# Values computed in pairs, early groups reordered, and some weight sums made by transfers

## The chip, the cores and the metric

The kernel runs on one core of one Trainium2 chip. The metric is the time of one execution on the device in microseconds (us); the time shown for a kernel is the median of several runs. All matrix products run in float32r on TensorE (PE). VectorE (DVE) and ScalarE (ACT) prepare operands and do the rest of the arithmetic, GpSimd (POOL) does a few small operations, and SyncE (SP) issues the loads.

## The reference, cut to what matters

The input x has 256 rows of 4096 numbers. One layer is computed:

```
xn   = rms_norm(x)
proj = xn @ w_in                      # 4096 x 14336, split into q, k, v, z_a, a, g, z_c (2048 columns each)
y_a  = rms_norm(chunked_attention(q, k, v, rel_table)) * silu(z_a)      # 16 heads of 128
u    = causal depthwise conv, 31 taps, of a * sigmoid(g)
y_c  = rms_norm(silu(layer_norm(u)) @ w_pw + b_pw) * silu(z_c)
h    = x + concat(y_a, y_c) @ w_out
h    = h + sigmoid(rms_norm(h) @ w_ple_gate + b) * (p @ w_ple)
out  = rms_norm(h)
```

## The kernel before

**Products.** Rows are two halves of 128 (h), columns are blocks of 512, the inner dimension is blocks of 128. Every operand is split into a high part (cast to float32r) and a low part (the rest), and each product is three matmuls: high x high, low x high, high x low. Weights are split on the core: ACT casts the high part (L204), DVE subtracts to get the low part (L205); both are made in `parts_of`.

**Units.** `mixed_product` computes two column blocks at a time. A unit is a pair of inner blocks. A plain unit takes 2 x 2 x 2 products of three matmuls, 24 in all. A unit marked `*` replaces eight products by seven (21 matmuls), in the manner of Strassen: it needs sums of the weight blocks, `ua` (two column-wise sums, L426 and L427) and `ub` (two more built on `ua`, L430 and L431), which are made on DVE, cast and split like weights (`pair_parts`), and matching combinations of the activations (`comb`, `xS`). The seven products go into the four accumulators and into four helper banks P1, P5, P6, P7, which are all four temporary banks of PSUM (`ps_tmp`). After the last seven of an order, `on_helpers` adds the helpers up. The orders are written by hand as text, such as `early`, with the `*` units among the plain ones.

**Fills.** Work with time to spare is queued in `later`: convolution taps (L677), the steps of the layer norm over the convolution, combinations. After each unit of a product, `fill(n)` takes n of them; the counts stand in `early_fills`, one for each unit. A compile-time scheduler then fixes each engine's order, mainly by program order and by the readiness that its model gives.

**Order of the first half.** `glu_conv(c)` computes a and g for 512 columns as a pair and queues 124 taps. `heads(g)` computes q and k for four heads as a pair (`scaled_pair`, q and k 2048 columns apart), turns both into head layout (`to_heads`), then computes v for these heads as one block of 512 columns with `product` (L218: no seven-product units, 192 matmuls), then `attention`. The order is conv group 0, then for g = 0, 1, 2: conv group g+1 and heads g; then the layer norm is queued and heads 3 follow. Before the last v product, the pool for sums (`upool`) is closed and a pool (`more`) takes its place, which holds the split operand of the pointwise product (`uS`). The pointwise product follows, with the orders "1 3 4 5 0* 6 2* 7" and plain.

**Attention** of one group runs four heads one after the other: scores on PE (L848, L849), bias, maximum and exponential on DVE and ACT (L855 to L860), transposes (L867), the product with v (L872 to L874), scaling into `y_a` (L876). Each head takes three banks from `ps_tmp`. The bias tile is loaded by SP at the start of `heads` and then partly overwritten by POOL (L895).

**Buffers that matter.** Weight tiles: 5 (`wpool`); their high and low parts: 3 each; `u` tiles and their parts: 2 each; tag `hd` (bias, kT, v, convolution inputs, layer norm scratch): 5; `ps_tmp` banks: 4. SP loads weights in order, each load waiting for a free tile.

Of the kernel before, what the change touches and what calls it, by code (L numbers as in the profile page):

```python
# [3 lines left out]

# [21 lines left out]
def hybrid_block(  # L26
# [23 lines left out]
    nc = tc.nc  # L50
# [113 lines left out]
    def transposed(src, blocks, then=lambda ins: None):  # L164

        pt = tmp_psum()
        for i, b in enumerate(blocks):
            for h in range(NH):
                last_transpose[:] = [
                    nc.tensor.transpose(  # L170
                        pt[:, i * T + h * P : i * T + (h + 1) * P],
                        src[:, h, b * P : (b + 1) * P],
                        ident,
                    )
                ]
                then(*last_transpose)
        return [pt[:, i * T : (i + 1) * T] for i in range(len(blocks))]
# [21 lines left out]
    def parts_of(wt, kc, tiles=None):  # L199
        if tiles is None:  # L200
            tiles = part_tiles()
        wh, wl = tiles
        made = (
            nc.scalar.copy(wh[:, :kc, :], wt[:, :kc, :]),  # L204
            nc.vector.tensor_tensor(  # L205
                wl[:, :kc, :], wt[:, :kc, :], wh[:, :kc, :].bitcast(F32), ALU.subtract
            ),
        )
        return (wh, wl), made

    def accumulate(acc, h, lhs, kb, wh, wl, k, kblocks, then=lambda ins: None):
        t, i = lhs[kb // 4], kb % 4
# [99 lines left out]

    def units(text):

        return [(int(u.rstrip("*")), u.endswith("*")) for u in text.split()]


    dense = units("1 0* 3 2* 5 4* 6* 7 8* 9 10* 11 12* 14* 13 15")
    first = units("0 1 3 5 7 9 11 13 15 2* 8 4* 10 6* 12 14")
    early = units("1 3 5 7 0* 9 2* 11 4* 13 6* 15 8 10 12 14")  # L320
    early_six = units("1 3 5 7 0* 9 2* 11 4* 13 6* 15 8* 10* 12 14")

    early_fills = (4, 6, 7, 1, 5, 1, 5, 1, 5, 1, 2, 4, 6, 6, 6, 4)
    final = units("1 0* 3 2* 5 4* 6* 7 8* 9 10* 12* 11 13 14 15")
    late = units("1 3 5 7 9 11 13 15 0* 2 4* 6 8* 10* 12 14")

    def mixed_product(
# [54 lines left out]
        def add_plain(n, k, wh, wl, **kw):  # L382
            pair = order[n][0]
            for j in range(2):
                for h in range(NH):
                    name = (("P2", "P3"), ("P4", "X"))[h][j]
                    add(name, block(2 * pair + k, h), (wh[:, j], wl[:, j]), n, k == 1, **kw)

        done, after = 0, ExitStack()
        if begin:  # L390
            done, behind = begin(add_plain)
# [3 lines left out]
        for n, (pair, seven) in enumerate(order):  # L395
# [4 lines left out]
            wts = []  # L400
            for k in range(2):
                wt = wpool.tile([P, 2, NB], F32, tag="w", name="wt")
                nc.sync.dma_start(wt, two_columns(w, 2 * pair + k, col, apart))
# [18 lines left out]
            ua = upool.tile([P, 2, NB], F32, tag="u", name="ua")  # L422
            ub = upool.tile([P, 2, NB], F32, tag="u", name="ub")
            plus = partial(nc.vector.tensor_tensor, op=ALU.add)
            w0h, w0l = parts_of(w0, 1)[0]
            plus(ua[:, 0], w0[:, 0], w0[:, 1])  # L426
            plus(ua[:, 1], w0[:, 1], w1[:, 1])  # L427
            uah, ual = pair_parts(ua)
            w1h, w1l = parts_of(w1, 2)[0]
            plus(ub[:, 0], ua[:, 0], w1[:, 1])  # L430
            plus(ub[:, 1], ub[:, 0], w1[:, 0])  # L431
            ubh, ubl = pair_parts(ub)
# [37 lines left out]
        tt(z[1][0], helper["P7"], z[1][0], ALU.add)  # L470
        tt(z[1][1], helper["P5"], z[1][0], ALU.add)

    def sum_tiles():

        t = [spool.tile([P, NH, NB], F32, tag="stage", name="z") for _ in range(2)]
        return t, [[t[j][:, h] for j in range(2)] for h in range(NH)]

    def scaled_pair(w, col, apart, order, r, fills, **kw):

        t, z = [], []  # L480

        def on_helpers(helper):
            for dst, src in zip((t, z), sum_tiles()):
                dst.extend(src)
            nc.scalar.activation(z[0][0], helper["P1"], AF.Identity, scale=r[:, :1])
            helper_sums(helper, z)
            for h, j in QUARTERS[1:]:
                nc.scalar.activation(z[h][j], z[h][j], AF.Identity, scale=r[:, h : h + 1])

        c = mixed_product(w, col, xT, xS, order, on_helpers, fills=fills, apart=apart, **kw)  # L490
        for h, j in QUARTERS:
            stt(  # L492
                z[h][j], c[h][j], r[:, h : h + 1], z[h][j],
                ALU.mult, ALU.subtract if j else ALU.add,
            )
        return t

    def square_sum(dst, src, scale=1.0):
        junk = spool.tile([P, NB], mybir.dt.bfloat16, tag="junk", name="junk", bufs=1)
        return nc.scalar.activation(junk[:, : src.shape[1]], src, AF.Square, scale=scale, accum_out=dst)  # L500

    def rstd_of(partial, n, name):
        r = cpool.tile([P, partial.shape[1]], F32, name=name)
# [185 lines left out]
    def glu_conv(c):  # L689
        if c == 0:  # L690
            sg, gate = scaled_pair(
                w_in0, o_a, o_g - o_a, first, r_x, (1,), begin=first_pairs
            )
        else:
            last = c == CW // NB - 1
            sg, gate = scaled_pair(
                w_in0, o_a + c * NB, o_g - o_a, early_six if last else early, r_x, early_fills,
                ahead=more_combinations if last else None,
            )
        for h in range(NH):  # L700
# [25 lines left out]
    def layer_norm_swish():  # L726

        add = nc.vector.tensor_tensor
        st = {}

        def hd_tile(name):
            return spool.tile([P, 4, T], F32, tag="hd", name=name, bufs=5)

        def fold(s):
            add(s[:, :2, :], s[:, :2, :], s[:, 2:, :], ALU.add)
# [87 lines left out]
    y_a = []  # L823
    ssq_a = cpool.tile([P, NH, AW // NB], F32, name="ssq_a")

    def to_heads(st, name):

        t = spool.tile([P, GH, T], F32, tag="hd", name=name, bufs=5)
        for pair in range(GH // 2):
            pt = tmp_psum()  # L830
            for i in range(2):
                for h in range(NH):
                    b = 2 * pair + i
                    nc.tensor.transpose(  # L834
                        pt[:, i * T + h * P : i * T + (h + 1) * P],
                        st[:, h, b * P : (b + 1) * P],
                        ident,
                    )
# [5 lines left out]
    def attention(g, qT, kT, v, bias):  # L844
        y = act.tile([P, NH, NB], F32, tag="act", name="y_a")
        for hd in range(GH):
            sp = tmp_psum()
            nc.tensor.matmul(sp[:, :P], qT[:, hd, :P], kT[:, hd, :P], start=True, stop=True)  # L848
# [25 lines left out]
            nc.tensor.matmul(o[:, HD : 2 * HD], pT[:, 2 * P :], v[:, 1, vc], start=False, stop=True)  # L874
            for h in range(NH):
                nc.scalar.activation(  # L876
                    y[:, h, vc], o[:, h * HD : (h + 1) * HD], AF.Identity, scale=den[:, h : h + 1]
                )
        for h in range(NH):
            square_sum(ssq_a[:, h, g : g + 1], y[:, h, :])  # L880
        y_a.append(y)

    def heads(g):
        nonlocal more
        bias = spool.tile([P, GH, T], F32, tag="hd", name="bias", bufs=5)
# [10 lines left out]
        q, k = scaled_pair(w_in0, o_q + g * NB, o_k - o_q, early, r_x, (4,) if g == n_g - 1 else early_fills)  # L896
        qT, kT = to_heads(q, "qT"), to_heads(k, "kT")
        if g == n_g - 1:
            first_sums.close()
            more = pool("more", 4)  # L900
        accv = product(w_in0, o_v + g * NB, xT, KD)
        v = spool.tile([P, NH, NB], F32, tag="hd", name="v", bufs=5)
        for h in range(NH):
            nc.scalar.activation(v[:, h, :], accv[h], AF.Identity, scale=r_x[:, h : h + 1])
        attention(g, qT, kT, v, bias)

    n_g = H // GH
    assert n_g == CW // NB
# [68 lines left out]
    def gated(ys, c0, col, r_y, order, ahead):  # L977
# [6 lines left out]

        acc = mixed_product(w_in0, col + c0 * NB, xT, xS, order, on_helpers, ahead=ahead, fills=(2,))
        for h, j in QUARTERS:
            zz, y = z[h][j], ys[c0 + j][:, h, :]
            tt(zz, acc[h][j], zz, ALU.subtract if j else ALU.add)  # L988
            nc.scalar.activation(zz, zz, AF.Silu, scale=r_x[:, h : h + 1])
            later.append(partial(stt, y, y, r_y[:, h : h + 1], zz, ALU.mult, ALU.mult))  # L990

    def before_last(make):
# [278 lines left out]
```

## Time and profile before

| | |
|---|---|
| median of 3 runs | 2038.79 us (2037.45 to 2039.75) |
| profiled execution | 2039.1 us, span 2037.3 us |
| PE busy | 2019.6 us, 9106 matmuls |
| DVE busy | 1887.9 us |
| ACT busy | 1200.8 us |
| POOL busy | 8.1 us, 19 instructions |
| moved by transfers | 412.29 MB |

The span is the time from the first to the last instruction of the one profiled execution; around it lie 1.8 us of that execution's own time. Engine times overlap. A line such as L370 is the line of the kernel's file; `acc` and `acc_P` are the accumulators and the helper banks of `mixed_product`, `wh` and `wl` high and low parts of weights, `uh` and `ul` those of the sums. PEld is PE's weight load.

### The profile page before, as it was taken

The page shows a single profiled execution, that of the slowest core. Times are in us where ns is not written, and L with a number is a line of the kernel's source. Part 1 is how long each engine was busy: PE and PEld are TensorE (multiplying, and loading weights), DVE is VectorE, ACT ScalarE, POOL GpSimd, SP SyncE. Part 2 cuts the span into 40 slices and gives each one's busy share as a digit, 9 for nine tenths or more (in the row PEclk, how much of TensorE's full clock was granted, in tenths as well). Part 3 has the DMA queues.
Part 4 walks back from the last instruction along what each step waited for, and adds up shares of the span by engine and source line. Part 5 has one row for each costly group of instructions (what it writes and reads, how often), then busy time and mean ns, then how long its engine had stood idle before and what let it go on. Part 6 is the DMA issues. An engine that isn't in the chain of part 4 may idle for free.

```text
span 2037.3 us, 26041 instructions
## 1 busy us (share of the span) xinstructions
PE 2019.6 (99%) x9106; PEld 1659.5 (81%) x9106; DVE 1887.9 (93%) x2688; ACT 1200.8 (59%) x1559; POOL 8.1 (0%) x19
## 2 busy tenths in 40 slices
PE   9999999999999999999999999999999999999997
PEld 7888888877888888888888888888888888888876
DVE  7999999799989998868899999999999999999998
ACT  7655546554565546676555656676565666655555
POOL 0000000000000000000000000000000000000000
PEclk9999999999999999999999999999999999999999
DMA  8666665666656665655666666676666656666765
GB/s 295 188 200 204 204 187 165 202 191 189 184 185 204 201 188 183 186 184 199 190 216 204 197 216 199 219 238 204 214 201 205 214 185 208 198 221 205 235 208 179
DMA packets 161853, 412.29 MB, mean 202 GB/s; under 512 B 12974, under 2 KB 16190, under 8 KB 161722
## 3 DMA queue, kind: packets, MB, share of 16 engines
q1 hardware_dynamic: 161072, 409.80, 63.3%
q8 instruction: 71, 1.16, 0.2%
q10 hardware_dynamic: 650, 0.84, 0.1%
q14 instruction: 60, 0.49, 0.1%
HBM read 406.39 MB, written 4.19 MB: 202 GB/s over the span
## 4 chain that ended last, share of the span: by engine, by line
PE 86%; DVE 10%; issue 2%; DMA 1%; ACT 1%; POOLq 0%; POOL 0%; ACTq 0%; DVEq 0%
PE acc L370 61%; PE acc_P L370 15%; PE acc L218 7%; DVE wl L205 4%; DVE cv L677 3%; DMA wt<-in_w_in_dram 1%; PE tmp_ps L170 1%; DVE ul L205 1%; PE tmp_ps L867 0%; PE tmp_ps L849 0%; ACT wh L204 0%; PE acc L358 0%; PE tmp_ps L834 0%; DVE z L492 0%; PE tmp_ps L872 0%
## 5 line engine op out<-in xcount | busy, mean ns | idle before, releaser
L370 PE MATMUL acc<-wh,big_t 128*128 128x512 f32 x3788 | 1172.1, 391 | 0.6 <-DVE z L988 0.3
L204 ACT CAST wh<-wt 128x1024 fp32r<-128x1024 f32 (+1 forms) x737 | 715.8, 982 | 543.0 <-PE acc L370 330.6
L205 DVE TENSOR_TENSOR wl<-wt,wh 128x1024 fp32r<-128x1024 f32 (+1 forms) x737 | 825.4, 1132 | 65.0 <-ACT wh L204 60.1
L370 PEld LDWEIGHTS acc<-wh,big_t 128*128 128x128 f32 x3788 | 708.4, 188 | 146.5 <-issue 0.6
L370 PE MATMUL acc<-wl,big_t 128*128 128x512 f32 x1894 | 731.1, 391 | 1.0 <-DVE wl L205 1.0
L370 PEld LDWEIGHTS acc<-wl,big_t 128*128 128x128 f32 x1894 | 355.2, 188 | 76.7 <-DVE wl L205 3.1
L677 DVE SCALAR_TENSOR_TENSOR cv<-uT,dw,cv 128x255 f32<-128x255 f32 (+23 forms) x480 | 204.9, 467 | 1.1
L204 ACT CAST uh<-ub 128x1024 fp32r<-128x1024 f32 x122 | 128.5, 1054 | 126.2 <-DVE ub L431 102.7
L218 PE MATMUL acc<-wh,big_t 128*128 128x512 f32 x560 | 173.1, 390 | 0.0
L204 ACT CAST uh<-ua 128x1024 fp32r<-128x1024 f32 x122 | 128.7, 1055 | 71.7 <-DVE ua L427 63.5
L205 DVE TENSOR_TENSOR ul<-ub,uh 128x1024 fp32r<-128x1024 f32 x122 | 149.0, 1221 | 8.8 <-ACT uh L204 7.8
L370 PE MATMUL acc_P<-uh,big_t 128*128 128x512 f32 x504 | 154.4, 392 | 0.0
L205 DVE TENSOR_TENSOR ul<-ua,uh 128x1024 fp32r<-128x1024 f32 x122 | 148.9, 1220 | 0.4 <-ACT uh L204 0.2
L218 PEld LDWEIGHTS acc<-wh,big_t 128*128 128x128 f32 x560 | 104.8, 188 | 21.4
L370 PEld LDWEIGHTS acc_P<-uh,big_t 128*128 128x128 f32 x504 | 93.3, 188 | 22.2 <-ACT uh L204 3.7
L218 PE MATMUL acc<-wl,big_t 128*128 128x512 f32 x280 | 109.1, 390 | 0.0
L426 DVE TENSOR_TENSOR ua<-wt 128x512 f32<-128x512 f32 x122 | 83.9, 688 | 25.9 <-DMA wt<-in_w_in_dram 19.0
L370 PE MATMUL acc_P<-ul,big_t 128*128 128x512 f32 x252 | 96.8, 392 | 0.0
L427 DVE TENSOR_TENSOR ua<-wt 128x512 f32<-128x512 f32 x122 | 83.7, 686 | 3.9 <-DMA wt<-in_w_in_dram 3.0
L431 DVE TENSOR_TENSOR ub<-ub,wt 128x512 f32<-128x512 f32 x122 | 83.8, 687 | 1.0
L430 DVE TENSOR_TENSOR ub<-ua,wt 128x512 f32<-128x512 f32 x122 | 83.7, 686 | 0.3
L370 PE MATMUL acc<-uh,big_t 128*128 128x512 f32 x244 | 75.4, 390 | 0.0
(241 smaller groups left out, 1523.0 us busy)
## 6 DMA issues: line engine op xcount, KB each, us to landing
wt<-in_w_in_dram SPq DMA_DIRECT2D x447, 512.0 KB, 4.0
wt<-in_w_out_dram SPq DMA_DIRECT2D x128, 512.0 KB, 4.2
wt<-in_w_ple_gate_dram SPq DMA_DIRECT2D x128, 512.0 KB, 4.2
wt<-in_w_pw_dram SPq DMA_DIRECT2D x32, 512.0 KB, 4.5
hc<-in_x_dram SPq DMA_DIRECT2D x8, 512.0 KB, 5.8
wt<-in_w_ple_dram SPq DMA_DIRECT2D x8, 512.0 KB, 4.2
xin<-in_x_dram SPq DMA_DIRECT2D x7, 512.0 KB, 8.2
out_dram<-hc SPq DMA_DIRECT2D x12, 256.0 KB, 2.4
```

The source lines that it names most:

```text
L170: nc.tensor.transpose(pt[:, i * T + h * P : i * T + (h + 1) * P], src[:, h, b * P : (b + 1) * P], ident,)
L204: nc.scalar.copy(wh[:, :kc, :], wt[:, :kc, :]),
L205: nc.vector.tensor_tensor(wl[:, :kc, :], wt[:, :kc, :], wh[:, :kc, :].bitcast(F32), ALU.subtract),
L218: nc.tensor.matmul(acc, a, b[:, k, :], start=kb == 0 and kind == 0, stop=kb == kblocks - 1 and kind == 2,)
L370: nc.tensor.matmul(banks[name], a, b, start=name not in begun, stop=final and ends[name] == n and kind == 2 and not (left and name in "P2 ...
L426: plus(ua[:, 0], w0[:, 0], w0[:, 1])
L427: plus(ua[:, 1], w0[:, 1], w1[:, 1])
L430: plus(ub[:, 0], ua[:, 0], w1[:, 1])
L431: plus(ub[:, 1], ub[:, 0], w1[:, 0])
L677: nc.vector.scalar_tensor_tensor(cv[:, i, PAD - k :], uT[:, i, : T + k - PAD], dw[:, b, k : k + 1], cv[:, i, PAD - k :], ALU.mult, ALU.add,)
```

## The change

- **Paired values.** v is no longer one column block per group with `product`. `values(g)` computes the v of groups g and g+1 as one pair with `scaled_pair`, with four seven-product units in each call. Their destination is given by `home` (for the first call the `hd` tag).
- **Order.** `heads` is taken apart into `load_bias`, `keys`, `values`, `attention`, which are now called as in the list below. Attention 2 and 3 stand together at the end, their biases are loaded inside the last values call, where the pool `more` is opened as well. Attention now writes its result over the q tile, in head layout, and later readers follow.
- **Early order.** The plain and seven-product units are mixed in another order, with other fill counts; the last conv group keeps the former counts (`six_fills`).
- **Transferred sums.** A unit marked `+` is a seven-product unit whose `ua` is not made by DVE: SP loads the shared second column block twice into `ua`, and a transfer issued by POOL adds the two other blocks onto it in the transfer (`accum_op=ALU.add`). It is asked for up to two units ahead (`sums_ahead`). The unit's first weight tile then loads one column block only, and `ub` is made in place in `ua`.
- **Queueing.** For `+` units, the cast and the low part of `ua` are put behind the last cast and low part of the preceding pair on their engines (`queued_behind`; ordering only).

```diff
-    early = units("1 3 5 7 0* 9 2* 11 4* 13 6* 15 8 10 12 14")
+    early = units("1 3 5 0+ 7 9 2+ 11 13 4+ 15 8 6+ 10 12 14")
+    valued = units("1 3 5 7 8 0+ 9 10 2+ 11 12 4+ 13 6* 14 15")
-    early_fills = (4, 6, 7, 1, 5, 1, 5, 1, 5, 1, 2, 4, 6, 6, 6, 4)
+    early_fills = (5, 6, 1, 5, 6, 1, 5, 6, 1, 5, 6, 1, 2, 5, 5, 4)
+    six_fills = (4, 6, 7, 1, 5, 1, 5, 1, 5, 1, 2, 4, 6, 6, 6, 4)
...
+    @contextmanager
+    def queued_behind(made):
+        with ExitStack() as queued:
+            for ins in made:
+                queued.enter_context(tc.issue_after(ins.ins))
+            yield
...
+        def sums_ahead(n):
+            for m in range(n, min(n + 3, len(order))):
+                if order[m][1] != "+" or m in sums:
+                    continue
+                ua = sums[m] = upool.tile([P, 2, NB], F32, tag="u", name="ua")
+                rows = w[2 * order[m][0] * P : (2 * order[m][0] + 1) * P, :]
+                step = P * rows.ap[0][0]
...
+                nc.sync.dma_start(ua, columns(col + apart, 0))
+                nc.gpsimd.dma_start(ua, columns(col, step + apart), accum_op=ALU.add)
...
+                if seven == "+" and k == 0:
+                    nc.sync.dma_start(wt[:, 0], w[2 * pair * P : (2 * pair + 1) * P, col : col + NB])
+                else:
+                    nc.sync.dma_start(wt, two_columns(w, 2 * pair + k, col, apart))
                 wts.append(wt)
+            sums_ahead(n)
...
+            before = list(recent)
             w0h, w0l = parts_of(w0, 1)[0]
-            plus(ua[:, 0], w0[:, 0], w0[:, 1])
-            plus(ua[:, 1], w0[:, 1], w1[:, 1])
-            uah, ual = pair_parts(ua)
+            if seven == "+":
+                ua = ub = sums[n]
+            else:
+                ua = upool.tile([P, 2, NB], F32, tag="u", name="ua")
+                plus(ua[:, 0], w0[:, 0], w0[:, 1])
+                plus(ua[:, 1], w0[:, 1], w1[:, 1])
+            with queued_behind(before if seven == "+" else ()):
+                uah, ual = pair_parts(ua)
...
-        y = act.tile([P, NH, NB], F32, tag="act", name="y_a")
+        y = qT.rearrange("q g (h d) -> q h g d", h=NH)
...
+    def values(g, order, fills, **kw):
+        vs[g], vs[g + 1] = scaled_pair(w_in0, o_v + g * NB, NB, order, r_x, fills, **kw)
+
+    def late_pool():
+        nonlocal more
+        first_sums.close()
+        more = pool("more", 4)
+        for g in (2, 3):
+            load_bias(g)
...
     glu_conv(0)
-    for g in range(n_g):
-        if g + 1 < n_g:
-            glu_conv(g + 1)
-        else:
-            layer_norm_swish()
-        heads(g)
+    glu_conv(1)
+    load_bias(0)
+    keys(0, early_fills)
+    values(0, early, early_fills, home=dict(tag="hd", bufs=5))
+    attention(0)
+    glu_conv(2)
+    glu_conv(3)
+    load_bias(1)
+    keys(1, early_fills)
+    attention(1)
+    keys(2, early_fills)
+    layer_norm_swish()
+    keys(3, (4,))
+    values(2, valued, (5, 5, 4, 5, 4, 1, 3, 2, 1, 3, 2, 1, 1, 6, 6, 6), then=late_pool)
+    attention(2)
+    attention(3)
```

More of the change, by code (lines that the diff above doesn't have):

```diff
@@ L387, in add_plain, with columns @@
                     add(name, block(2 * pair + k, h), (wh[:, j], wl[:, j]), n, k == 1, **kw)
+        sums = {}
+        def sums_ahead(n):
[5 more added lines that the diff above has]
+                step = P * rows.ap[0][0]
+                def columns(first, step):
+                    return bass.AP(
+                        tensor=rows.tensor, offset=rows.offset + first,
+                        ap=[list(rows.ap[0]), [step, 2], [1, NB]],
+                    )
+                nc.sync.dma_start(ua, columns(col + apart, 0))
+                nc.gpsimd.dma_start(ua, columns(col, step + apart), accum_op=ALU.add)
         done, after = 0, ExitStack()
@@ L471, in helper_sums, with sum_tiles, scaled_pair @@
         tt(z[1][1], helper["P5"], z[1][0], ALU.add)
-    def sum_tiles():
-        t = [spool.tile([P, NH, NB], F32, tag="stage", name="z") for _ in range(2)]
+    def sum_tiles(**kw):
+        kw = kw or dict(tag="stage")
+        t = [spool.tile([P, NH, NB], F32, name="z", **kw) for _ in range(2)]
         return t, [[t[j][:, h] for j in range(2)] for h in range(NH)]
-    def scaled_pair(w, col, apart, order, r, fills, **kw):
+    def scaled_pair(w, col, apart, order, r, fills, home={}, then=lambda: None, **kw):
         t, z = [], []
         def on_helpers(helper):
-            for dst, src in zip((t, z), sum_tiles()):
+            for dst, src in zip((t, z), sum_tiles(**home)):
                 dst.extend(src)
+            then()
             nc.scalar.activation(z[0][0], helper["P1"], AF.Identity, scale=r[:, :1])
@@ L696, in glu_conv @@
             sg, gate = scaled_pair(
[L697 removed]
+                w_in0, o_a + c * NB, o_g - o_a, *((early_six, r_x, six_fills) if last else (early, r_x, early_fills)),
                 ahead=more_combinations if last else None,
@@ L876, in attention, with hd_tile, load_bias @@
                 nc.scalar.activation(
-                    y[:, h, vc], o[:, h * HD : (h + 1) * HD], AF.Identity, scale=den[:, h : h + 1]
+                    y[:, h, hd], o[:, h * HD : (h + 1) * HD], AF.Identity, scale=den[:, h : h + 1]
                 )
         for h in range(NH):
-            square_sum(ssq_a[:, h, g : g + 1], y[:, h, :])
+            square_sum(ssq_a[:, h, g : g + 1], y[:, h])
         y_a.append(y)
-    def heads(g):
-        nonlocal more
-        bias = spool.tile([P, GH, T], F32, tag="hd", name="bias", bufs=5)
+    qs, ks, vs, biases = {}, {}, {}, {}
+    def hd_tile(name):
+        return spool.tile([P, GH, T], F32, tag="hd", name=name, bufs=5)
+    def load_bias(g):
+        bias = biases[g] = hd_tile("bias")
         span = 2 * MAXR + 1
@@ L895, in heads, with keys @@
         nc.gpsimd.memset(bias[: P // 2, :, : P // 2], NEG)
[L896 to L905, printed above, removed]
+    def keys(g, fills):
+        q, k = scaled_pair(w_in0, o_q + g * NB, o_k - o_q, early, r_x, fills)
+        qs[g] = act.tile([P, GH, T], F32, tag="act", name="qT")
+        to_heads(q, qs[g])
+        ks[g] = hd_tile("kT")
+        to_heads(k, ks[g])
+    def values(g, order, fills, **kw):
[6 more added lines that the diff above has]
+            load_bias(g)
     n_g = H // GH
-    assert n_g == CW // NB
+    assert n_g == CW // NB == 4
     glu_conv(0)
-    for g in range(n_g):
-        if g + 1 < n_g:
-            glu_conv(g + 1)
-        else:
-            layer_norm_swish()
-        heads(g)
+    glu_conv(1)
[14 more added lines that the diff above has]
+    attention(3)
     r_a = rstd_of(ssq_a, AW, "r_a")
```

28 lines of the change are left out of this document (15 added, 13 removed).

## The prediction

> **What bounds the kernel now.** I read the page's totals first, then the chain of waits in order of time, then what TensorE waited for, then busy time by stage.
>
> ```profile
> span 2037.3 us, 26041 instructions
> PE 2019.6 (99%) x9106; PEld 1659.5 (81%) x9106; DVE 1887.9 (93%) x2688; ACT 1200.8 (59%) x1559; POOL 8.1 (0%) x19
> PEclk9999999999999999999999999999999999999999
> PE 86%; DVE 10%; issue 2%; DMA 1%; ACT 1%; POOLq 0%; POOL 0%; ACTq 0%; DVEq 0%
> ...
> q1 hardware_dynamic: 161072, 409.80, 63.3%
> ```
>
> TensorE (PE) is busy for 2019.6 of 2037.3 us at full granted clock. So all idle time together is 17.7 us, and whatever is saved on VectorE (DVE), ScalarE (ACT) or the transfers can return at most that. The other way to save is fewer matmuls, so their price matters. One uninterrupted run in the chain gives it, the second values product:
>
> ```profile
> 499.47 43.55 PE acc L218 x192
> ```
>
> 43.55 / 192 = 0.2268 us for each matmul of 512 columns. Next, what PE waited for, by its weight loads:
>
> ```profile
> PEld acc_P L370 <- ACT uh L204: 4.7, 18, 0.5
> PEld tmp_ps L867 <- ACT s L860: 4.1, 12, 0.7
> PEld acc_P L370 <- DVE ul L205: 4.0, 14, 0.6
> PEld tmp_ps L872 <- ACT pT L869: 3.4, 11, 0.4
> PEld acc L370 <- DVE wl L205: 3.1, 7, 1.2
> PEld tmp_ps L834 <- DVE z L492: 3.1, 5, 1.7
> ```
>
> These are many short waits: 11.8 us for prepared weights (uh, ul, wl) over the whole kernel, 10.6 us inside attention and at its transposes. By stage:
>
> ```profile
> 102.00:316.00 214.00, 213.88 (x957) 175.88 (x957) 213.40 (x352) 106.33 (x117) 0.31 (x1) 1.00 0.65 199
> 860.00:904.00 44.00, 44.00 (x198) 36.50 (x197) 32.61 (x58) 31.19 (x53) 0.00 (x0) 1.00 0.62 190
> 904.00:932.00 28.00, 28.00 (x144) 22.63 (x143) 17.19 (x36) 20.20 (x45) 1.06 (x1) 1.00 0.47 156
> 58.00:1080.00 1022.00, 1018.22 (x4600) 836.10 (x4599) 928.03 (x1436) 573.79 (x744) 4.69 (x8) 1.00 0.62 192
> ```
>
> The columns are window, length, then busy us (count) of PE, PEld, DVE, ACT, POOL, then clock, DMA share and GB/s. From 102 to 316 us DVE is as full as PE (213.4 of 214), yet PE loses nothing: the convolution taps are what gets put off. Later DVE has gaps. The changed half, 58 to 1080 us, has PE idle for 3.8 us by this count. The end of the chain is PE.
>
> **Part 1: values in pairs (the only PE term).** A plain unit (two row blocks by two column blocks) is 24 matmuls, a seven-product unit 21. The four single products are 4 x 32 x 2 x 3 = 768 matmuls. Two paired calls of 16 units with four sevens each are 2 x (384 - 12) = 744. The other groups keep their counts: the early order has four sevens before and after, the last gate group keeps six. So 24 matmuls go: 24 x 0.2268 = **-5.4 us**. All of this is on the path, because PE is.
>
> Its cost lies on DVE, priced from these rows:
>
> ```profile
> L205 DVE TENSOR_TENSOR wl<-wt,wh 128x1024 fp32r<-128x1024 f32 x44 | 53.5, 1220 | 0.2 <-ACT wh L204 0.2
> L205 DVE TENSOR_TENSOR wl<-wt,wh 128x512 fp32r<-128x512 f32 x4 | 2.8, 690 | 0.0
> L205 DVE TENSOR_TENSOR ul<-ua,uh 128x1024 fp32r<-128x1024 f32 x4 | 4.9, 1222 | 0.0
> L426 DVE TENSOR_TENSOR ua<-wt 128x512 f32<-128x512 f32 x4 | 2.8, 688 | 0.0
> L427 DVE TENSOR_TENSOR ua<-wt 128x512 f32<-128x512 f32 x4 | 2.8, 690 | 0.0
> L492 DVE SCALAR_TENSOR_TENSOR z<-acc,r_x,z 128x512 f32<-128x512 f32 x32 | 22.4, 750 | 4.9 <-PE acc L370 4.9
> L468 DVE TENSOR_TENSOR z<-acc_P,z 128x512 f32<-128x512 f32 x20 | 13.8, 688 | 1.7 <-PE acc_P L370 1.2
> L677 DVE SCALAR_TENSOR_TENSOR cv<-uT,dw,cv 128x255 f32<-128x255 f32 (+23 forms) x480 | 204.9, 467 | 1.1
> ```
>
> Plain unit: 2 x 1.22 = 2.44 us. Seven with sums on DVE: 0.69 + 3 x 1.22 + 4 x 0.69 = 7.1. Seven with the first two sums transferred: 7.1 - 1.38 = 5.7. The values now hold 24 plain, 7 transferred and 1 other seven: 58.6 + 39.9 + 7.1 = 105.6 us, against 32 x 2.44 = 78.1 before, so +27.5. Each pair ends with four helper sums and four scaled sums, 2 x 4 x (0.69 + 0.75) = +11.5 us.
>
> **Part 2: transferred sums and the new order.** There are 31 transferred units (seven calls of the early order with four each, three in the last values call), 24 of them outside the values: -24 x 1.38 = -33.1 us of DVE. Net DVE: 27.5 + 11.5 - 33.1 = **+5.9 us**. On the path I cost it at nothing: the row of 58 to 1080 us shows DVE idle for 94 us, and 934 of 1017 us remain covered. Without that cover it would cost up to 5.9.
>
> The order helps local balance. Before, a seven alternates with a plain unit: DVE 7.1 + 2.44 + 6 taps x 0.467 = 12.3 us against PE's 45 x 0.2268 = 10.2, four times in a row, 8.4 us of backlog. After, each three units hold one seven and 12 taps: 2 x 2.44 + 5.7 + 5.6 = 16.2 against 69 x 0.2268 = 15.6, four times, 2.4 us. That could take back part of the 11.8 us of weight waits, but those rows count the untouched second half too. I take 0 and keep -6 for the range.
>
> ```profile
> L204 ACT CAST uh<-ua 128x1024 fp32r<-128x1024 f32 x122 | 128.7, 1055 | 71.7 <-DVE ua L427 63.5
> ```
>
> ACT gets one and a half casts more per seven in the values, 1.5 x 1.055 x 8 = 13 us, plus a few copies. It is busy 573.8 of 1022 us in this half, so nothing on the path.
>
> Queueing the sums' cast and low part behind the preceding pair adds no instruction. Behind a waiting cast stand all later casts on ACT and then PE's next weights, so this edge costs nothing only while the sum has landed in time.
>
> **Part 3: the transfers and their queues.**
>
> ```profile
> wt<-in_w_in_dram SPq DMA_DIRECT2D x447, 512.0 KB, 4.0
> bias<-in_rel_table_dram SPq DMA_DIRECT2D x4, 512.0 KB, 5.9
> xin<-in_x_dram SPq DMA_DIRECT2D x7, 512.0 KB, 8.2
> SPq L403 <- DVE wl L205: 1052.4, 478, 9.8
> ```
>
> Today loads are paced by free buffers: SP's queue waited 1052 us for the split that frees a weight tile. The price of 512 KB on all engines is 0.633 x 2037.3 us / 409.80 MB x 0.524 MB = 1.65 us. A transferred unit drops half a load (-0.83), adds a plain one (+1.65) and an accumulating one of unknown price a. No accumulating transfer is in this trace. A lower bound for a is the plain 1.65. An upper one is the slowest landing of such a tile, 8.2 us, taken as if it filled all engines. I take 3.3 us, an old and a new operand moved, nearest to the plain row. Early groups then hold 32 x 1.65 + 4 x (0.82 + 3.3) = 69.3 us of transfers in 372 x 0.2268 = 84.4 us of PE, 82% (63% now). The bounds are 74% and 105%.
>
> [...]
>
> Timing: the sum is requested before the unit two ahead is computed, and that unit's weights are themselves loaded about two units early. This gives some 4 x 5.2 = 21 us for two landings in a row, 8 to 16 us by the rows above. So no wait, at nothing on the path; if the cover goes, each late us is paid up to 31 times. POOL's queue, with 19 operations now, gets 31 transfers, beside four bias memsets and the small powers: one behind a memset waits a bias landing, 5.9 us, within the slack.
>
> **Part 4: moved attention.** Attention of groups 2 and 3 now stand together behind the last values, ahead of the pointwise product. Their bias loads move past the weights of 14 units to unit 6*, with two plain units (10.9 us) over their 5.9 us. The pool for the conformer operand opens only there, so by the fill counts 12 of its 16 splits stay queued for behind attention. Attention's length:
>
> ```profile
> 903.65 0.38 PE L848 MATMUL tmp_ps<-kT,qT 128*128 128x128 f32 x2
> 926.46 0.63 ACT L876 ACTIVATE y_a<-tmp_ps,den 128x128 f32<-128x128 f32 x2 [1.14 <-PE tmp_ps L874]
> ```
>
> Four heads in a row take 23.4 us; PE fills them with the next group's plain units until the first seven needs the four temporary banks. From the row of 904 to 932 us, some 95 large matmuls take 21.5 us and 49 small ones the other 6.5, so four heads hold 52 x 0.133 = 6.9 us of PE. Two attentions: 46.8 us long, with 13.8 us of their own and four plain pointwise units (21.8) to fill: 11 us uncovered at worst. At best nothing: the first head's scores need no values and can run under units 14 and 15, and heads go faster when fewer casts interrupt them. Elsewhere the early order now starts with three plain units: 16.3 + 6.9 = 23.2 against 23.4, still covered. I take 0 here, nearest to the 904 to 932 row, where PE was full, and keep +11.
>
> **The sum.** 2039.1 (profiled execution, span 2037.3) - 5.4 = 2033.7; the median shown, 2038.8, lies 0.3 lower, so **2033.4 us**.
>
> **Rivals.** *Heads run out of cover* (same or slower): the two attentions leave PE idle. For it: only four plain units before the banks are needed, with splits queued behind. Against: PE was full in every attention window. All 11 us: 2033.4 + 11 = 2044. It eats the gain at 5.4 us and is a loss beyond 0.2% from 9.5 us.
>
> *Transfers bind* (slower): in three units the engines carry 4 x 1.65 + 0.83 + 1.65 + 1.65 + a = 10.7 + a against 15.6 us; from a = 4.9 us they are late within a run, from 7.1 us over a group. At 8.2 us each group is 4.5 us over, times 31/4: 2033.4 + 35 = 2068. For: share above 80%, two landings in a row, ACT in order behind it. Against: loads wait for buffers now.
>
> *Smoother DVE* (faster): half of the 11.8 us of weight waits also goes: 2033.4 - 6 = 2027.
>
> *The sums are never the point*: if DVE's sums were covered anyway, parts 2 and 3 are worth nothing and part 1 alone stands: the forecast itself.
>
> **How the numbers follow.** Measurements of this kernel can tell about 0.2%, 4.1 us. Forecast with at most 1.3 us of loss: 0.43. Smoother DVE: 0.13. Partly uncovered heads, within 0.2%: 0.22. Fully uncovered: 0.10. Transfers bind: 0.12. Faster: 0.43 + 0.13 = 0.56; same 0.22; slower 0.22. The range goes from the smoother case, 2026, to just past full uncovering, 2046; what binding transfers give lies outside.
>
> **What would show it.** PE with 24 matmuls fewer (9082) and no L218 accumulation in this half; DVE about 6 us busier; sums' casts without waits for transfers; DMA share from 0.65 to near 0.8 in early groups; PE full where attentions 2 and 3 run. Wrong if ACT waits long for ua from a transfer, if SP's waits turn from buffers to landings, or if PE shows gaps of over 1 us before the pointwise product.

## The result and the profile after

The changed kernel takes 2052.38 us (median of 4 runs, 2051.01 to 2052.80) against 2038.92 us for the kernel before: ratio 1.0064, 95% interval 1.0052 to 1.0077. It is slower by 13.5 us, where 5.4 us less was forecast. The page of the changed kernel, its totals, chain, transfer queues and the issues of the sums (KB each, us to landing):

```profile
span 2049.2 us, 26149 instructions
PE 2020.4 (99%) x9082; PEld 1655.8 (81%) x9082; DVE 1893.2 (92%) x2690; ACT 1207.1 (59%) x1575; POOL 46.0 (2%) x50
...
q1 hardware_dynamic: 158240, 417.93, 62.8%
q0 software_dynamic: 8432, 16.25, 4.8%
...
PE 89%; DVE 5%; issue 2%; ACT 2%; DMA 1%; POOL 0%; POOLq 0%; ACTq 0%; DVEq 0%
...
ua<-in_w_in_dram SPq DMA_DIRECT2D x31, 512.0 KB, 4.2
ua<-in_w_in_dram POOLq DMA_DIRECT2D x31, 512.0 KB, 8.5
```

Much came as forecast: 9082 matmuls, DVE up by 5.3 us (5.9 forecast), POOL with 31 instructions more. But PE's busy time did not fall, in part because matmuls take longer where the clock falls: in the row from 525 to 530 us below, at a clock of 0.75, 17 of them fill 4.84 us, where 17 x 0.2268 us would be 3.9. And PE's idle time rose from 17.7 to 28.8 us. The windows of the changed kernel (window, length, busy us and count of PE, PEld, DVE, ACT, POOL, clock, DMA share, GB/s) show where:

```profile
382.00:465.00 83.00, 83.00 (x372) 68.74 (x371) 60.09 (x73) 44.27 (x49) 1.88 (x2) 1.00 0.70 208
465.00:520.00 55.00, 54.62 (x236) 43.16 (x235) 54.74 (x84) 30.07 (x34) 0.00 (x0) 1.00 0.59 182
520.00:525.00 5.00, 2.62 (x9) 1.81 (x9) 5.00 (x9) 2.59 (x4) 0.00 (x0) 0.91 0.41 124
525.00:530.00 5.00, 4.84 (x17) 3.38 (x16) 5.00 (x8) 1.04 (x1) 0.14 (x1) 0.75 0.68 219
530.00:550.00 20.00, 18.63 (x84) 14.51 (x83) 20.00 (x35) 11.21 (x14) 2.60 (x3) 1.00 0.91 249
...
892.00:906.00 14.00, 7.76 (x40) 5.25 (x39) 11.89 (x32) 13.78 (x37) 0.00 (x0) 1.00 0.21 72
906.00:940.00 34.00, 34.00 (x180) 27.48 (x179) 23.66 (x54) 25.03 (x64) 0.00 (x0) 1.00 0.37 125
```

**Two places, not one spread loss.** The first is the last gate group, now directly behind another gate group (465 to 550 us): DVE has almost no idle time, PE stands still for 2.4 us at 520 us, and the clock is granted at 0.91 and 0.75 in the two rows there (at 0.53 in a window from 524 to 526 us alone: the half clock of the expectations below). The group before it leaves DVE idle for 23 of 83 us, because the queue of taps had run empty (no tap runs from 355 to 450 us). The stop at 520 us, on DVE, ACT and PE:

```profile
519.67 0.47 DVE L723 SCALAR_TENSOR_TENSOR cv<-uT,dw,cv 128x247 f32<-128x247 f32 x1
520.05 0.68 DVE L466 TENSOR_TENSOR ua<-wt 128x512 f32<-128x512 f32 x1
520.66 0.46 DVE L723 SCALAR_TENSOR_TENSOR cv<-uT,dw,cv 128x246 f32<-128x246 f32 x1
521.04 0.68 DVE L467 TENSOR_TENSOR ua<-wt 128x512 f32<-128x512 f32 x1
...
521.81 1.04 ACT L204 CAST uh<-ua 128x1024 fp32r<-128x1024 f32 x1 [1.31 <-DVE ua L467]
...
522.91 1.19 PE L384 MATMUL acc_P<-uh,comb_x 128*128 128x512 f32 x4 [2.38 <-ACT uh L204]
```

PE waits for the cast of a sum, and the cast waits for DVE, which makes the sum late, with taps (L723) between its two halves. The second place is the beginning of attention 2 (892 to 906 us): PE works 7.8 of 14 us, with ACT full. Behind it, from 906 to 940 us, PE is full, although attentions 2 and 3 are running and only four plain pointwise units are at hand.

### The profile page after: what moved, and what is told of

Same layout as the page of the kernel before. It is cut to its first block, busy times and chain, and to the rows that moved or that the text cites. A ratio compares the mean times of both kernels' runs of the same rounds, so it can differ in the third digit from the quotient of the medians.

```text
span 2049.2 us, 26149 instructions
## 1 busy us (share of the span) xinstructions
PE 2020.4 (99%) x9082; PEld 1655.8 (81%) x9082; DVE 1893.2 (92%) x2690; ACT 1207.1 (59%) x1575; POOL 46.0 (2%) x50
## 3 DMA queue, kind: packets, MB, share of 16 engines
q1 hardware_dynamic: 158240, 417.93, 62.8%
## 4 chain that ended last, share of the span: by engine, by line
PE 89%; DVE 5%; issue 2%; ACT 2%; DMA 1%; POOL 0%; POOLq 0%; ACTq 0%; DVEq 0%
PE acc L384 69%; PE acc_P L384 16%; DVE wl L205 2%; DVE cv L723 1%; DMA wt<-in_w_in_dram 1%; PE tmp_ps L170 1%; PE acc L229 1%; DVE ul L205 1%; ACT cv L835 0%; ACT wh L204 0%; PE tmp_ps L876 0%; PE tmp_ps L892 0%; DMA wt<-in_w_out_dram 0%; PE tmp_ps L915 0%; PE tmp_ps L910 0%
## 5 line engine op out<-in xcount | busy, mean ns | idle before, releaser
L384 PE MATMUL acc<-wh,big_t 128*128 128x512 f32 x4196 | 1295.9, 391 | 4.0 <-ACT wh L204 1.8
L204 ACT CAST wh<-wt 128x1024 fp32r<-128x1024 f32 (+1 forms) x737 | 711.7, 976 | 567.0 <-PE acc L384 421.5
L384 PE MATMUL acc<-wl,big_t 128*128 128x512 f32 x2098 | 806.8, 391 | 1.3 <-DVE wl L205 1.3
L384 PEld LDWEIGHTS acc<-wl,big_t 128*128 128x128 f32 x2098 | 393.2, 188 | 85.4 <-DVE wl L205 3.9
L204 ACT CAST uh<-ua 128x1024 fp32r<-128x1024 f32 x161 | 169.2, 1051 | 71.8 <-DVE ua L467 50.4
L723 DVE SCALAR_TENSOR_TENSOR cv<-uT,dw,cv 128x250 f32<-128x250 f32 (+26 forms) x480 | 204.9, 462 | 1.0
L205 DVE TENSOR_TENSOR ul<-ua,uh 128x1024 fp32r<-128x1024 f32 x161 | 196.3, 1219 | 7.3 <-ACT uh L204 6.7
L204 ACT CAST uh<-ub 128x1024 fp32r<-128x1024 f32 x99 | 104.2, 1052 | 106.3 <-DVE ub L474 91.1
L466 DVE TENSOR_TENSOR ua<-wt 128x512 f32<-128x512 f32 x99 | 68.0, 687 | 20.6 <-DMA wt<-in_w_in_dram 14.1
L384 PE MATMUL acc_P<-wh,big_t 128*128 128x512 f32 x260 | 80.4, 389 | 0.0
L467 DVE TENSOR_TENSOR ua<-wt 128x512 f32<-128x512 f32 x99 | 67.8, 685 | 3.6 <-DMA wt<-in_w_in_dram 2.4
L384 PE MATMUL acc_P<-uh,comb_t 128*128 128x512 f32 x228 | 70.0, 391 | 0.1
L474 DVE TENSOR_TENSOR ub<-ub,wt 128x512 f32<-128x512 f32 x99 | 67.9, 686 | 0.8
L384 PEld LDWEIGHTS acc_P<-ul,big_t 128*128 128x128 f32 x264 | 49.1, 188 | 14.5 <-DVE ul L205 4.2
```

Of the source, the lines that this page charges most:

```text
L205: nc.vector.tensor_tensor(wl[:, :kc, :], wt[:, :kc, :], wh[:, :kc, :].bitcast(F32), ALU.subtract),
L384: nc.tensor.matmul(banks[name], a, b, start=name not in begun, stop=final and ends[name] == n and kind == 2 and not (left and name in "P2 ...
L723: nc.vector.scalar_tensor_tensor(cv[:, i, PAD - k :], uT[:, i, : T + k - PAD], dw[:, b, k : k + 1], cv[:, i, PAD - k :], ALU.mult, ALU.add,)
```

## The experiments

Median, ratio to the kernel before (runs on the same chip) and its interval. The kernel before took 2038.5 to 2039.6 us on the chips used, so about 1 us between two versions tells nothing:

| version | us | ratio | 95% interval |
|---|---|---|---|
| change | 2052.4 | 1.0064 | 1.0052 to 1.0077 |
| dve_sums | 2057.0 | 1.0087 | 1.0072 to 1.0102 |
| gate_apart | 2043.1 | 1.0020 | 1.0011 to 1.0029 |
| pool_early | 2045.3 | 1.0031 | 1.0019 to 1.0042 |
| both | 2038.0 | 0.9991 | 0.9982 to 1.0000 |
| sums_only | 2038.8 | 1.0002 | 0.9992 to 1.0011 |
| six_transferred | 2049.1 | 1.0053 | 1.0038 to 1.0068 |
| not_queued | 2080.5 | 1.0205 | 1.0189 to 1.0221 |
| fills_moved | 2045.9 | 1.0032 | 1.0018 to 1.0046 |
| spread | 2034.9 | 0.9981 | 0.9972 to 0.9990 |
| spread_dve | 2046.5 | 1.0038 | 1.0023 to 1.0053 |
| spread_even | 2039.3 | 1.0003 | 0.9994 to 1.0013 |
| spread_thin | 2044.3 | 1.0025 | 1.0014 to 1.0035 |
| spread_late | 2032.6 | 0.9963 | 0.9948 to 0.9977 |

### Are the transfers the loss?

**dve_sums**, all sums back on DVE:

```diff
-    early = units("1 3 5 0+ 7 9 2+ 11 13 4+ 15 8 6+ 10 12 14")
-    valued = units("1 3 5 7 8 0+ 9 10 2+ 11 12 4+ 13 6* 14 15")
+    early = units("1 3 5 0* 7 9 2* 11 13 4* 15 8 6* 10 12 14")
+    valued = units("1 3 5 7 8 0* 9 10 2* 11 12 4* 13 6* 14 15")
```

> The changed kernel with every transferred sum made on DVE again (31 units go back to DVE sums; everything else is kept). Theory of the two stalls (time was lost in the last gate group and at the two attentions, the transfers cost nothing): DVE gets 31 x 1.38 = 43 us more to do, so no faster than the changed kernel: 2052 to 2065 us. Rival, transfers in the way (accumulating transfers slow the loads): at least half of the loss goes, 2040 to 2046 us.

2057.0 us: slower by 4.6 us than the change (the two intervals overlap slightly). The transfers are not what is lost; if anything they help. That clears the rival of binding transfers, and so does the changed kernel's own trace, where ACT never waited for a sum to land.

**sums_only**, the transferred sums and the early order in the old sequence of groups with single values products:

```diff
+    def heads(g):
+        load_bias(g)
+        keys(g, (4,) if g == n_g - 1 else early_fills)
...
+        accv = product(w_in0, o_v + g * NB, xT, KD)
...
+    glu_conv(0)
+    for g in range(n_g):
+        if g + 1 < n_g:
+            glu_conv(g + 1)
+        else:
+            layer_norm_swish()
+        heads(g)
```

> The kernel before, with its order of groups and its single values products, but with the early order, the fill counts and the transferred sums of the change (24 transferred units, no pairs of values). Two stalls (transfers cost nothing): DVE is relieved by 33 us and no group is moved, so 2032 to 2039 us. Rival, transfers in the way: 2042 us or more.

2038.8 us, the same as before. In that sequence the transfers and the early order together cost nothing and bring nothing, although its page shows DVE busy for 1860.3 us instead of 1887.9: DVE was covered there. What each of the two does alone was not measured.

**not_queued**, the ordering edge left out:

```diff
-            with queued_behind(before if seven == "+" else ()):
+            with queued_behind(()):
```

> The changed kernel without the ordering edge of the transferred sums: their cast and low part are placed where the compile-time scheduler likes. Two stalls: the edge costs nothing, within 3 us of 2052. Rival, the edge holds casts back: faster by over 4 us, under 2048.

2080.5 us, 28 us worse, against both expectations: I had thought the edge worth nothing. Without it the compile-time order puts the sums' casts earlier, and ACT then waits for transfers with the other casts behind it. Two rows of ACT's waits in this version (total, times, longest):

```profile
ACT uh L204 <- DVE ua L474: 61.6, 22, 6.4
ACT uh L204 <- DMA ua<-in_w_in_dram: 16.1, 3, 7.1
```

The second row shows 16.1 us in three waits for transfers; the changed kernel has no such row. The first is larger: casts of the second sums (L474) wait 61.6 us for DVE, against 16.3 us in the changed kernel. How these waits add up to the 28 us, with PE waits on casts and low parts all through the early groups, was not taken apart.

### The last gate group

**gate_apart** puts this group back behind attention 1:

```diff
     glu_conv(2)
-    glu_conv(3)
     load_bias(1)
     keys(1, early_fills)
     attention(1)
+    glu_conv(3)
     keys(2, early_fills)
```

> The changed kernel with the last gate group put back between attention 1 and the third keys, as in the kernel before, so that it no longer follows another gate group directly. Two stalls: the waits of about 8 us between 500 and 550 us, half clock included, go, the waits at the two attentions stay: 2043 to 2047 us. Rival, transfers in the way: the same transfers run, so within 2 us of 2052. Rival, banks run out: within 2 us of 2052.

2043.1 us: 9.3 us come back, at the favourable end of what the theory of the two stalls said. Its window over attention 1 and most of that gate group:

```profile
550.00:635.00 85.00, 84.61 (x384) 68.78 (x384) 83.11 (x127) 53.51 (x72) 2.44 (x2) 1.00 0.70 209
```

PE is full again at full clock. DVE is nearly as full as in the change, but the group's first units now run under attention 1. From its first combination (L277) to its last sigmoid (L747) the group now takes 82.6 us instead of 70.1, so DVE has 12.5 us longer for it while PE has attention to do.

**fills_moved** leaves the group where the change put it and moves half of its taps:

```diff
-    six_fills = (4, 6, 7, 1, 5, 1, 5, 1, 5, 1, 2, 4, 6, 6, 6, 4)
+    six_fills = (2, 3, 3, 1, 2, 1, 2, 1, 2, 1, 1, 2, 3, 3, 3, 2)
-    keys(3, (4,))
+    keys(3, (6,))
```

> The changed kernel with 32 of the 64 convolution taps that are filled into the last gate group moved to the third-last stage (keys of group 3, two more after each unit). Taps that crowd DVE as the cause of the waits at 500 to 550 us: 15 us less for DVE there, the waits and the half clock go, 2044 to 2048 us. Rival, the order of the casts and sums themselves in that group (six sevens with DVE sums and two combinations): the waits stay above 5 us, 2049 to 2054 us.

2045.9 us, 6.5 us back, as the crowding of DVE by taps would have it. The group's window holds 35 taps instead of 52, and the clock stays at 1.00:

```profile
465.00:550.00 85.00, 83.50 (x368) 67.66 (x367) 82.30 (x121) 46.93 (x54) 2.74 (x3) 1.00 0.72 222
```

**six_transferred** takes 8.3 us of sums from DVE in the same group:

```diff
-    early_six = units("1 3 5 7 0* 9 2* 11 4* 13 6* 15 8* 10* 12 14")
+    early_six = units("1 3 5 7 0+ 9 2+ 11 4+ 13 6+ 15 8+ 10+ 12 14")
```

> The changed kernel with the six sevens of the last gate group transferred as well (8.3 us less for DVE in that group, six transfers more). Backlog of DVE as the cause of the waits at 500 to 550 us: they shrink from 8 us to under 3, no half clock, 2044 to 2048 us. Rival, another cause there (late combinations, late loads): within 2 us of 2052, or slower.

2049.1 us: only 3.2 us back, between the two expectations. Its windows:

```profile
465.00:505.00 40.00, 39.47 (x172) 31.68 (x171) 34.97 (x54) 19.19 (x22) 2.48 (x3) 1.00 0.77 221
505.00:550.00 45.00, 40.52 (x174) 31.19 (x173) 43.43 (x68) 25.38 (x30) 5.12 (x5) 1.00 0.87 244
```

The relief went into the first 40 us, where DVE now idles; from 505 us DVE is crowded as before and PE loses 4.5 us. The half clock is gone: the second row reads 1.00, where the change reads 0.96 over the same 45 us. So less DVE work is not enough, its place counts too. Why the compile-time order still bunches it there was not settled.

### The two attentions

**pool_early** moves the last seven of the second values call from unit 14 to unit 11, so that the pool for the pointwise operand opens five units before the end:

```diff
-    valued = units("1 3 5 7 8 0+ 9 10 2+ 11 12 4+ 13 6* 14 15")
+    valued = units("1 3 5 0+ 7 8 2+ 9 10 4+ 6* 11 12 13 14 15")
...
-    values(2, valued, (5, 5, 4, 5, 4, 1, 3, 2, 1, 3, 2, 1, 1, 6, 6, 6), then=late_pool)
+    values(2, valued, (5, 5, 5, 1, 6, 6, 1, 6, 6, 1, 1, 5, 5, 5, 5, 4), then=late_pool)
```

> The changed kernel with the sevens of the last values call moved forward (last one at unit 11 of 16 instead of 14), so that the pool for the pointwise operand opens five units before the end and all its splits are filled in ahead of attention 2. Two stalls, with the queued splits as the cause at the attentions: PE gaps between 890 and 906 us go, 2040 to 2044 us. Rival, banks run out (only four plain pointwise units before the helper banks are needed): the gaps move behind the fourth unit and stay, 2050 to 2053 us. Rival, transfers in the way: sevens stand closer, so 2052 or more.

2045.3 us, 7.1 us back, somewhat less than expected. The number of plain pointwise units is the same, so running out of banks is not the cause. From 885 to 915 us PE is now busy without a gap. **both** joins this edit to that of gate_apart:

> Both edits together: last gate group apart, sevens of the last values call forward. Two stalls: the two gains add up and the 24 matmuls saved show, 2032 to 2037 us. Rivals (transfers in the way, banks run out): 2048 to 2053 us.

2038.0 us, just above the range expected: the gains nearly add up (14.4 of 9.3 + 7.1), but the saved matmuls still do not show in full. Its trace has waits left around 870 us. **spread** therefore keeps attentions 2 and 3 apart:

```diff
     glu_conv(3)
+    load_bias(2)
     keys(2, early_fills)
+    values(2, early, early_fills, home=dict(tag="hd", bufs=5))
+    attention(2)
     layer_norm_swish()
-    keys(3, (4,))
-    values(2, valued, ..., then=late_pool)
-    attention(2)
+    keys(3, (5, 5, 5, 1, 6, 6, 1, 6, 6, 1, 2, 6, 6, 6, 5, 4), valued, then=late_pool)
     attention(3)
...
```

It has gate_apart's order and pool_early's order of units, here used by the last keys call.

> A version that keeps all of the change but spreads the attentions: last gate group after attention 1, second values call and attention 2 ahead of the layer norm and the third keys (no: the keys of group 3), whose sevens are moved forward so that the pool opens five units before attention 3. Two stalls, with crowding of the layer norm's tail and the attentions as cause: PE is full at both attentions and the 24 matmuls show in full, 2030 to 2035 us. Rival, the remaining 10 us of waits in the version with both edits belong to the transfers or the tail itself: 2036 to 2040 us.

2034.9 us, 0.2% faster than the kernel before and within the range, but not quite for the reason expected: from 860 to 900 us PE is busy for 37.8 of 40 us, not full. **spread_dve** is this version with all sums on DVE, the edit of dve_sums:

> The spread version with every transferred sum made on DVE again: pairs of values and the new order alone, 43 us more for DVE. If DVE's cover was enough without the transfers (as the prediction had it), within 2 us of the spread version: 2033 to 2037 us. If the pairs need the transfers to stay hidden: 2038 to 2045 us, the gain of the pairs gone.

2046.5 us, above the range expected: without the transfers the pairs lose 7.6 us against the kernel before. From 102 to 550 us, first with transfers, then without:

```profile
102.00:550.00 448.00, 447.77 (x2031) 369.83 (x2031) 415.64 (x667) 240.85 (x296) 22.57 (x20) 1.00 0.77 226
```

```profile
102.00:550.00 448.00, 446.78 (x2018) 367.55 (x2016) 432.54 (x692) 239.96 (x294) 0.61 (x2) 1.00 0.63 195
```

So the transfers are worth 11.6 us with the pairs in this sequence. In sums_only, without the pairs, transfers and early order together were worth nothing; but its sequence of groups differs too, so that the pairs alone make this difference is not shown.

### What stops PE there: ACT makes no casts

In the kernel before, the swish steps (L792) of the layer norm come a few at a time, with casts (L204) between them. From its ACT timeline:

```profile
862.46 1.59 ACT L792 ACTIVATE cv<-cv,prm 128x256 f32<-128x256 f32 x3
863.95 1.04 ACT L204 CAST wh<-wt 128x1024 fp32r<-128x1024 f32 x1
864.89 1.09 ACT L792 ACTIVATE cv<-cv,prm 128x256 f32<-128x256 f32 x2
865.89 1.04 ACT L204 CAST wh<-wt 128x1024 fp32r<-128x1024 f32 x1
866.84 2.08 ACT L792 ACTIVATE cv<-cv,prm 128x256 f32<-128x256 f32 x4
```

In the changed kernel (swish L835, splits L845, attention L903) they stand in a block:

```profile
882.21 1.05 ACT L204 CAST wh<-wt 128x1024 fp32r<-128x1024 f32 x1
...
888.40 5.02 ACT L835 ACTIVATE cv<-cv,prm 128x256 f32<-128x256 f32 x10
893.33 1.03 ACT L204 CAST wh<-wt 128x1024 fp32r<-128x1024 f32 x1
894.26 1.09 ACT L835 ACTIVATE cv<-cv,prm 128x256 f32<-128x256 f32 x2
895.26 1.31 ACT L845 CAST big_t<-cv 128x256 fp32r<-128x256 f32 x4
...
904.83 1.05 ACT L204 CAST wh<-wt 128x1024 fp32r<-128x1024 f32 x1
```

From one weight cast to the next it takes 11.1 us, then 11.5. There are three tiles of prepared weights, each good for 12 matmuls, 3 x 12 x 0.2268 = 8.2 us. Then PE has nothing but attention, whose own steps queue on ACT as well. PE's waits in the changed kernel from 780 to 960 us (total, times, longest):

```profile
PE tmp_ps L910 <- ACT s L903: 3.3, 4, 2.0
PE acc L384 <- ACT wh L204: 1.8, 1, 1.8
PE tmp_ps L915 <- ACT pT L912: 1.1, 2, 0.6
```

These three rows are the 6.2 us that PE stands still from 892 to 906 us. Waiting for a weight cast is 1.8 us of it; the rest is attention waiting for its own steps on ACT, which stand among the splits (all 16 run from 895.3 to 904.5 us). Only when a cast comes at last, at 904.83 us, do the pointwise units start and cover attention. pool_early, with the splits done earlier, has still a wait for a weight cast, but its longest wait for L903 is 0.4 us. What is left is the gap between casts, and three fill schedules of the spread version try this:

```diff
-    keys(3, (5, 5, 5, 1, 6, 6, 1, 6, 6, 1, 2, 6, 6, 6, 5, 4), valued, then=late_pool)
+    keys(3, (5, 6, 6, 1, 7, 7, 1, 7, 7, 1, 4, 4, 4, 4, 4, 3), ...)     # spread_even
+    keys(3, (7, 7, 7, 7, 7, 4, 4, 4, 4, 4, 2, 3, 3, 3, 3, 2), ...)     # spread_thin
+    keys(3, (5, 5, 5, 1, 6, 6, 1, 5, 4, 1, 4, 4, 4, 4, 4, 12), ...)    # spread_late
```

> The spread version with the fills of its last keys call changed (55 before the pool opens, 16 after, instead of 42 and 29), so that the splits are spread over six units. If the 7 us of waits that the spread version has more than the kernel before between 800 and 1000 us come from the queued tail of the layer norm: 2030 to 2033 us. If they come from the order of casts around attention itself: within 1.5 us of 2035.

> The spread version with the layer norm's steps filled in earlier, so that the 16 swish steps are spread over four units with weight casts between them (in the spread version they run within 10 us, and ACT makes no weight cast for 9.7 us; in the version with even fills for 12.4 us). If PE waits there because the swish burst on ACT shuts out the casts for longer than the three prepared weight tiles last (3 x 12 x 0.2268 = 8.2 us): the gap between casts falls to 7 us or less and the time to 2031 to 2033.5 us. If the waits come from the order around attention itself: 2034 to 2036 us.

> The spread version with the fills changed the other way: 39 steps before the pool opens, then four swish steps after each of four units, twelve splits after the last. In the three spread versions so far ACT made no cast for 9.7, 12.4 and 13.6 us around the swish burst, and PE waited 1.2, 3.3 and 5.4 us for a cast there. If PE's wait is that gap less the 8.2 us that three prepared tiles last: a gap of at most 8.5 us, no such wait, 2031 to 2034.5 us. If the fills do not move the burst: gap and wait as in the spread version, 2034 to 2036 us.

The first two missed: 2039.3 and 2044.3 us, worse than spread. Asking for the steps earlier does not thin the block. All swish steps wait for one statistic (L784, at 881.93 us in the change, at 866.33 in spread_thin and at 864.03 in spread_late, each time just ahead of the block) and become ready together, and those that are ahead in program order then pass the casts. spread_thin's ACT, and what PE's weight loads waited for in it:

```profile
866.62 1.05 ACT L204 CAST wh<-wt 128x1024 fp32r<-128x1024 f32 x1
867.68 1.28 ACT L835 ACT_TABLE_LOAD   x1
868.98 8.00 ACT L835 ACTIVATE cv<-cv,prm 128x256 f32<-128x256 f32 x16
876.88 1.93 ACT L533 ACTIVATE z<-z,r_x 128x512 f32<-128x512 f32 x3
878.72 1.61 ACT L845 CAST big_t<-cv 128x256 fp32r<-128x256 f32 x5
880.24 1.04 ACT L204 CAST wh<-wt 128x1024 fp32r<-128x1024 f32 x1
```

```profile
PEld acc L384 <- ACT wh L204: 5.4, 1, 5.4
```

Placed behind later units instead, the steps leave room. spread_late's ACT and PE wait:

```profile
864.31 1.05 ACT L204 CAST wh<-wt 128x1024 fp32r<-128x1024 f32 x1
...
870.50 2.06 ACT L835 ACTIVATE cv<-cv,prm 128x256 f32<-128x256 f32 x4
872.47 1.04 ACT L204 CAST wh<-wt 128x1024 fp32r<-128x1024 f32 x1
```

```profile
PEld acc L384 <- ACT wh L204: 0.5, 2, 0.3
```

The same row for spread and for spread_even, over the same window of 780 to 960 us (total, times, longest):

```profile
PEld acc L384 <- ACT wh L204: 2.6, 2, 1.4
```

```profile
PEld acc L384 <- ACT wh L204: 3.6, 1, 3.6
```

| version | from cast to cast, us | less 8.2 | longest wait of PE's weight loads for a cast |
|---|---|---|---|
| spread_late | 8.2 | 0.0 | 0.3 |
| spread | 9.7 | 1.5 | 1.4 |
| pool_early | 10.6 | 2.4 | 1.7 |
| change | 11.1 | 2.9 | 2.2 |
| spread_even | 12.4 | 4.2 | 3.6 |
| spread_thin | 13.6 | 5.4 | 5.4 |

The wait is the gap less what the prepared tiles last, to within 0.7 us. The times of the versions differ by more than these waits (spread_thin takes 9.4 us more than spread): part of that is the lower clock behind a wait (0.54 in spread_thin from 881 to 886 us, shown at the end), and the rest was not taken apart. spread_late takes 2032.6 us, 7 us less than the kernel before on its chip (ratio 0.9963, 0.9948 to 0.9977), and beats both kernels. The interval holds the 5.4 us of the matmuls, and its page shows PE busy for 2013.7 us, 5.9 us less than before.

## Why the prediction was wrong

**Part 1 was right in its term.** 24 matmuls are gone, and the gain of spread_late, where the stalls are nearly gone, fits what they were forecast to be worth. In the change they are outweighed by 19 us of waits and of matmuls at a lower clock (0.53 from 524 to 526 us). The two edits that answer parts 2 and 4 return 14.4 of these 19 us together (both).

**Part 2 failed in its cover.** I set "on the path nothing" against 94 us of DVE idle time in the whole first half. That is an average over stages with different limits. In the change one gate group has 23 us of DVE to spare and the next has none. What failed was not costing the move of this group at all: the section on moved work dealt with the attentions, their bias loads and splits, not with the gate group put directly behind another one with six sevens on DVE and 64 taps by its fill counts. Undoing that move alone returns 9.3 us. The rival "the sums are never the point" was wrong too: without transferred sums the pairs lose in the sequence of spread (spread_dve). For the ordering edge I had asked only what it costs; what it prevents is worth 28 us (not_queued).

**Part 3 held.** I took 3.3 us for the accumulating transfer, an estimate of mine: twice the plain 1.65 us, on the supposition that an old and a new operand move. 4.8% x 2049.2 us / 31 = 3.2 us were measured, and a plain 512 KB now takes 0.628 x 2049.2 / 417.93 x 0.524 = 1.6 us, so the accumulating one took twice the plain one. The page shows that time and not its cause: whether a second operand moves was not shown. The landing of 8.5 us was just above my bound of 8.2, and the lead covered it. The chance of 0.12 for transfers that bind was my estimate as well.

**Part 4 had the right place, but I took the wrong end of the range.** I kept "0 to 11 us" for the two attentions and chose 0, by the row of the kernel before. Opening the pool earlier (pool_early) returns 7 us. That this lies between 0 and 11 is luck, since I had worked the range out from another cause. The mechanism I named (helper banks, only four plain units) was not it, although the gaps of over 1 us that I had named as a sign did show: PE was full from 906 us on, through the other heads of attention 2 and all of attention 3. The 12 splits that I had counted as queued were the clue. With the swish block they kept ACT from casting the pointwise weights, so those plain units could not start, and they held up attention's own steps on ACT. I had dismissed ACT by its share of busy time, 573.8 of 1022 us, and not asked how long it may go without a cast.

## What to carry to other kernels

Look for the cover of moved work in the stage where it lands, not in the average of the engine: one group here had 23 us of DVE to spare and its neighbour none. An engine that feeds the bound one may be idle for much of the time (ACT was busy for 59%) and still stop it, if a block of other work on its queue lasts longer than the prepared buffers; compare the longest gap between two feeding instructions with what the buffers last (11.1 and 11.5 us against 8.2 in the change). Price the parts of a change together as well as alone: transfers and early order were worth 0 us in the old sequence, and the transfers 12 us in a sequence with the pairs.

## What the runs showed of the hardware

PE's clock fell after one short gap. In the changed kernel PE idled for 2.4 us at 520 us, and the clock rows read 0.91 from 520 to 525 us and 0.75 from 525 to 530. In spread_thin, around the wait of 5.4 us (PE idle for 5.0), they read:

```profile
870.00:881.00 11.00, 6.33 (x28) 4.82 (x26) 7.69 (x17) 11.00 (x24) 0.00 (x0) 0.90 0.16 50
881.00:886.00 5.00, 4.63 (x11) 3.23 (x12) 4.69 (x7) 4.94 (x12) 0.00 (x0) 0.54 0.40 109
```

So this wait cost more than its own length: the 11 matmuls behind it took 4.63 us, where 11 x 0.2268 would be 2.5. In the changed kernel the gap of 2.4 us was followed by a lower clock, while the gaps of up to 2.0 us between 892 and 904 us were not (their row reads 1.00). What tells the two apart was not settled.
